# Mixers of a hybrid decoder layer: TensorE's order written by hand, substitution for two heads at a time

## The chip, the core and the metric

The kernel runs on one core of one Trainium2 chip, as one program. The metric is the time of one execution in microseconds of the device, as the median of several runs; a second number comes from one execution that was profiled. The core has a matrix engine (TensorE, PE in the profile; its weight loads are PEld), a vector engine (VectorE, DVE), a scalar engine (ScalarE, ACT), a general engine (GpSimd, POOL) and a queue from which the transfers are issued (SyncE, SP). Each works through its own instructions in their order and waits on semaphores for the others.

## What is computed

One layer of a decoder for 1,024 prompt tokens and 8 x 8 sampled tokens, all in 32-bit floats:

```
x = x + 1/2 * post1(SwiGLU_1(pre1(x)))
h = pre2(x); z = h @ w_in                       # q, k, v; conv q/k/v; z; a, b; two gates
A: sliding-window (128) attention, 8 heads of 64, 2 key/value heads, a sink per head
B: conv of width 4 on q/k/v + SiLU, gated DeltaNet (4 heads of 128), gated RMSNorm
m = (sigmoid(gA) * (oA @ w_branch_a) + sigmoid(gB) * (oB @ w_branch_b)) @ w_out
x = x + post2(m)
x = x + 1/2 * post3(SwiGLU_2(pre3(x)))
```

The delta net needs, for each head and each block of tokens, the solution of a unit lower triangular system: with `a = I + M`, `M` strictly lower, it uses the inverse of `a`. The state then goes through the blocks one after another (the recurrence).

## The kernel before

The residual stream lies transposed (features on partitions, tokens along the free axis) in three chunks of 384, 384 and 320 tokens (`CH`). A product in 32-bit precision is made of three faster ones: weights and activations are split into a high and a low piece (`split_w`: a cast on ScalarE at L113 and a subtraction on VectorE at L114), and `gemm` (lines 140 to 142) multiplies high by high, high by low and low by high. `unit(u)` loads and splits 128 columns of `w_in`; a unit for all three chunks is 3 x 8 x 3 = 72 products. The mixers have 32 such units behind the ones for attention's q, k, v: 12 convolutions (`conv_unit`), 4 for z (`z_unit`), 16 gates (`gate_unit`, `gate_do`). Their results go to memory (`zd`, `gd`) or to a head's tiles.

Instructions are put in order by a planner at build time: it simulates all engines, and on each engine takes the next instruction that it believes ready, earlier program text first; `high_priority` moves some ahead. It thus decides where TensorE does a projection between two steps of attention or of the delta net. Only in attention did the program add edges of its own (`chain`, "halves in turn").

`attention_prompt` goes through 16 items (8 blocks of 128 queries x 2 pairs of heads). `att_s` makes the scores, VectorE adds the mask (L862) and takes maxima (L822), ScalarE the exponentials (L828), then four ScalarE multiplications divide by the sum (L832). `att_o` transposes the probabilities (L883), ScalarE copies them (L888), and TensorE multiplies by the values (L893). `attention_sample` does four such items for the sampled tokens.

`delta_head(h, A, ps)` does one head. Two sets of eight tiles, `HA` and `YA`, serve heads 0, 2 and 1, 3; `YA` is also attention's. Its parts:

- transposes of k and their squares for the norm (L1075 to L1078), the decay matrices: differences on VectorE (L1105), exponentials on ScalarE (L1113, L1114), their transposes on TensorE (L1119); q.k products (L1102) and k.k products (L1122), which give `M` (L1126), the last block by L1138 to L1152;
- the inverse of the 32 x 32 diagonal blocks: the blocks go to memory and come back one to a partition (`bd`, L1161 to L1165), 34 partitions; 31 steps of a multiplication and a subtraction on VectorE (L1180, L1186); a transposed copy (L1189); blocks out (L1187, L1190) and, into zeroed tiles `L` and `U` (POOL, L1191 and L1192), ten transfers back (L1195 to L1198);
- the inverse of 128 from 32, on TensorE (L1211 to L1230), scalings (L1202, L1203), and `M` turned into what the recurrence needs (L1235);
- the recurrence over 8 blocks (L1253 to L1272), in each a chain PE, DVE, PE, DVE;
- the sampled tokens (L1282 to L1306) and the gated norm (L1313 to L1323), whose result goes to `obd`.

The order of the calls is: attention; convolutions and z of head 0; `delta_head(0)`; and so on, four heads, with gates between and after; the last four gates go chunk by chunk, so that the chunks of `xn2` come free one by one for the next stage, which loads `oad` and `obd` (L1367).

PSUM tiles are `pa` (3, projections), `ph` and `py` (2 each; `pb` takes them in turn) and `po` (1).

Of the kernel before, what the change touches and what calls it, by code (L numbers as in the profile page):

```python
# [35 lines left out]
def body(ctx: ExitStack, tc: tile.TileContext, d):  # L36
# [23 lines left out]
    bd = [dp.tile([34, 32, 32], F32, tag=f"bd{i}", name=f"bd{i}") for i in range(12)]  # L60
# [758 lines left out]
    def softmax(s3, sk, sm):  # L819
        j = s3.shape[1]  # L820
        m, neg, e, l, r = (sm[:, 4 * i : 4 * i + j] for i in range(5))
        nc.vector.tensor_reduce(out=m, in_=s3, op=ALU.max, axis=AX.X)  # L822
        nc.vector.tensor_tensor(out=m, in0=m, in1=sk, op=ALU.max)
        nc.vector.tensor_tensor(out=e, in0=sk, in1=m, op=ALU.subtract)
        nc.vector.tensor_scalar_mul(neg, m, -1.0)
        nc.scalar.activation(e, e, AF.Exp)
        for i in range(j):
            nc.scalar.activation(s3[:, i, :], s3[:, i, :], AF.Exp, bias=neg[:, i : i + 1], accum_out=l[:, i : i + 1])  # L828
        nc.vector.tensor_tensor(out=l, in0=l, in1=e, op=ALU.add)
        nc.vector.reciprocal(r, l)  # L830
        for i in range(j):
            nc.scalar.mul(s3[:, i, :], s3[:, i, :], r[:, i : i + 1])  # L832

    items = [(n, tp2) for n in range(8) for tp2 in range(2)]
    pos = {}
    masked = []
    SYNC = mybir.DependencyInfo(mybir.DependencyClass.Sync, mybir.DependencyReason.DATA)
    NOSYNC = mybir.DependencyInfo(mybir.DependencyClass.NoSync, mybir.DependencyReason.DATA)
    chain = []
    half2 = (slice(0, 64), slice(64, 128))  # L840

    def att_s(it):
        n, tp2 = items[it]
        k0 = 128 if n == 0 else 0
        ps = (ph(), py())
        for j in range(2):
            for g2, hs in enumerate(half2):
                mm = nc.tensor.matmul(
                    ps[g2][:, j * 256 + k0 : j * 256 + 256],
                    YA[tp2 * 2 + j][hs, n * P : n * P + P],  # L850
                    kT[hs, (n - 1) * P + k0 : (n + 1) * P],
                    start=True,
                    stop=True,
                )
                if masked:
                    tc.add_manual_dep(mm.ins, masked[-1], SYNC, reason="both halves start together")
                if chain:
                    tc.add_manual_dep(mm.ins, chain[-1], NOSYNC, reason="halves in turn")
                chain.append(mm.ins.name)
        s4 = sbs[it % 2][:, :1024].rearrange("p (h k) -> p h k", k=256)[:, :, k0:256]  # L860
        for g2 in range(2):
            mask = nc.vector.tensor_tensor(  # L862
                out=s4[:, 2 * g2 : 2 * g2 + 2, :],
                in0=ps[g2].rearrange("p (j k) -> p j k", k=256)[:, :, k0:256],
                in1=cst[:, C_AM + k0 : C_AM + 256].unsqueeze(1).to_broadcast([P, 2, 256 - k0]),
                op=ALU.add,
            )
        masked.append(mask.ins.name)
        softmax(s4, vec[:, V_SK + 4 * tp2 : V_SK + 4 * tp2 + 4], st())

    def att_o(it):
        n, tp2 = items[it]
        sb = sbs[it % 2]
        if n not in pos:
            pos[n] = po_tile()
        po = pos[n]
        h2s = (1,) if n == 0 else (0, 1)
        pt = (ph(), py())
        for g2 in range(2):
            for h2 in h2s:  # L880
                for j in range(2):
                    c0 = (2 * g2 + j) * 256 + h2 * P
                    mm = nc.tensor.transpose(pt[g2][:, h2 * 256 + j * P : h2 * 256 + j * P + P], sb[:, c0 : c0 + P], ident)  # L883
                    tc.add_manual_dep(mm.ins, chain[-1], NOSYNC, reason="behind the scores")
                    chain.append(mm.ins.name)
        ptb = pts[it % 2]
        copies = [
            nc.scalar.copy(ptb[:, g2 * 512 + h2s[0] * 256 : g2 * 512 + 512], pt[g2][:, h2s[0] * 256 : 512]) for g2 in range(2)  # L888
        ]
        for h2 in h2s:  # L890
            blk = n - 1 + h2
            for g2, hs in enumerate(half2):
                mm = nc.tensor.matmul(  # L893
                    po[hs, tp2 * 256 : tp2 * 256 + 256],
                    vtok[:, blk * P + hs.start : blk * P + hs.stop],
                    ptb[:, g2 * 512 + h2 * 256 : g2 * 512 + h2 * 256 + 256],
                    start=h2 == h2s[0],
                    stop=h2 == 1,
                )
                tc.add_manual_dep(mm.ins, copies[1].ins.name, SYNC, reason="both halves start together")  # L900
                tc.add_manual_dep(mm.ins, chain[-1], NOSYNC, reason="halves in turn")
                chain.append(mm.ins.name)
        if tp2 == 1:
            for t in range(4):
                nc.scalar.copy(YA[t][:, n * P : n * P + P], po[:, t * P : t * P + P])

    def attention_prompt():
        for it in range(len(items)):
            att_s(it)
            if it > 0:  # L910
                att_o(it - 1)
        att_o(len(items) - 1)
        for t in range(4):
            nc.sync.dma_start(oad[t, :, :NPR], YA[t][:, :NPR])

    def attention_sample():
        kc, vc = YA[5], YA[7]
        nc.sync.dma_start(vc[:, :NPR].rearrange("p (b c) -> p b c", c=P), d["vc"].rearrange("b k c -> k b c"))
        nc.sync.dma_start(kc[:, :NPR].rearrange("p (b c) -> p b c", c=P), d["kc"])
        pos = po_tile()  # L920
        for it in range(4):
            bg2, g2 = it // 2, it % 2
            lo, hi = 64 * g2, 64 * g2 + 64
            ps = py()
            for b4 in range(4):
                b = bg2 * 4 + b4
                ql = qs[lo:hi, b, :, :].rearrange("p t k -> p (t k)")
                nc.tensor.matmul(ps[32 * b4 : 32 * b4 + 32, 0:128], ql, kc[lo:hi, b * P : b * P + P], start=True, stop=True)
                nc.tensor.matmul(ps[32 * b4 : 32 * b4 + 32, 128:192], ql, kT[lo:hi, NPR:NT], start=True, stop=True)
            sb = YA[6][:, it * 256 : it * 256 + 192]  # L930
            nc.vector.tensor_tensor(out=sb[:, 0:128], in0=ps[:, 0:128], in1=cst[:, C_SMC : C_SMC + P], op=ALU.add)
            nc.vector.tensor_tensor(
                out=sb[:, 128:192], in0=ps[:, 128:192], in1=cst[:, C_SMN + bg2 * NSM : C_SMN + bg2 * NSM + NSM], op=ALU.add
            )
            softmax(sb.unsqueeze(1), vec[:, V_SKS + g2 : V_SKS + g2 + 1], st())
            pt = py()
            nc.tensor.transpose(pt[:, 0:128], sb[:, 0:128], ident)
            nc.tensor.transpose(pt[:NSM, 128:256], sb[:, 128:192], ident)
            ptb = YA[0][:, it * 256 : it * 256 + 256]
            nc.scalar.copy(ptb[:, 0:128], pt[:, 0:128])  # L940
            nc.scalar.copy(ptb[:NSM, 128:256], pt[:NSM, 128:256])
            nc.tensor.matmul(
                pos[lo:hi, bg2 * 128 : bg2 * 128 + 128], vts[:, lo:hi], ptb[:NSM, 128:256], start=True, stop=False
            )
            for b4 in range(4):
                b = bg2 * 4 + b4
                nc.tensor.matmul(
                    pos[lo:hi, bg2 * 128 + 32 * b4 : bg2 * 128 + 32 * b4 + 32],
                    vc[:, b * P + lo : b * P + hi],
                    ptb[:, 32 * b4 : 32 * b4 + 32],  # L950
                    start=False,
                    stop=b4 == 3,
                )
        obs = YA[1][:, :256]
        nc.vector.tensor_copy(
            obs.rearrange("p (t b k) -> p t b k", t=4, b=8), pos[:, :256].rearrange("p (b t k) -> p t b k", t=4, b=8)
        )
        nc.sync.dma_start(oad[:, :, NPR:NT].rearrange("t p q -> p t q"), obs.rearrange("p (t q) -> p t q", t=4))


    ncv = s2b.tile([P, 12, 3], F32, tag="ncv", name="ncv")
    nc.vector.memset(ncv, 0.0)

    def conv_unit(u, dst):
        w = unit(U_QKV + u, f"qkv{u}")
        cw = [vec[:, V_CW + u * 4 + j : V_CW + u * 4 + j + 1] for j in range(4)]
        for c, (a, b) in enumerate(CH):
# [4 lines left out]
            gemm(ps, w, xn2, c)  # L972
# [39 lines left out]
    eps4 = s2b.tile([P, 1], F32, tag="eps4", name="eps4")  # L1012
    nc.vector.memset(eps4, 4.0 * P * EPS * EPS)

# [324 lines left out]
    for i in range(0, 2):  # L1339
        gate_unit(i)  # L1340
# [210 lines left out]
```

## Time and profile before

| | |
|---|---|
| median of 3 runs | 2436.82 us (2432.78 to 2436.84) |
| profiled execution | 2440.89 us, span of its instructions 2439.1 us |
| PE busy / PEld busy | 2373.7 us (97%) / 2291.1 us (94%) |
| DVE / ACT / POOL busy | 1704.9 us (70%) / 1127.3 us (46%) / 50.9 us (2%) |
| mean granted TensorE clock | 0.989 |
| transfers | 264.67 MB, 109 GB/s |
| the mixers as treated here | 855 to 1478 us of the span |

Rows of a stretch give, for each engine, busy microseconds and the number of instructions in brackets, then the granted TensorE clock (PEclk, 1.00 is full), the busy share of the transfer engines and GB/s. Rows of a group give line, engine, operation, the tiles written and read, shapes and count, then busy time and the mean of one in ns, then the idle time just before and what ended it. Rows of waits give who waited for whom: microseconds in total, times, the longest. Rows of the timeline give start, duration, engine, line and operation. Matmuls overlap in the record, so PE's busy time is not PE at its peak.

### The profile page before, as it was taken

How to read it: one execution, taken by the hardware profiler on the slowest of the kernel's cores; microseconds unless marked ns; L12 is line 12 of the kernel's file. 1: busy time of each engine (PE TensorE's matmuls, PEld its weight loads, DVE VectorE, ACT ScalarE, POOL GpSimd, SP SyncE). 2: the span in 40 equal slices, each digit the busy share in tenths (PEclk: the TensorE clock that was granted, in tenths of full speed). 3: DMA queues.
4: the chain of work that ended last, by engine and by line, in shares of the span. 5: the costliest groups of instructions: out<-in, count | busy, mean ns of one | idle time of the engine just before them, and what ended most of it. 6: DMA issues, size and time to landing. Idle time of an engine off the chain costs nothing.

```text
span 2439.1 us, 38987 instructions
## 1 busy us (share of the span) xinstructions
PE 2373.7 (97%) x14535; PEld 2291.1 (94%) x14535; DVE 1704.9 (70%) x3519; ACT 1127.3 (46%) x2344; POOL 50.9 (2%) x36
## 2 busy tenths in 40 slices
PE   8999999999999999989999999999999999999997
PEld 7999999999998988888898899999999999999997
DVE  8887657757788576679697226556997576676677
ACT  7644423323465478634544333246654333233344
POOL 0000000000000000011111000000000000000000
PEclk9999999999999999999999999999999999999998
DMA  8332212213453311322223345435532122122453
GB/s 270 121 117 87 69 51 86 70 51 96 166 187 125 123 40 46 105 75 85 94 79 102 94 157 167 130 117 204 164 98 93 57 74 78 52 78 81 154 166 132
DMA packets 161558, 264.67 MB, mean 109 GB/s; under 512 B 35028, under 2 KB 66232, under 8 KB 161360
## 3 DMA queue, kind: packets, MB, share of 16 engines
q1 hardware_dynamic: 161368, 262.18, 33.3%
q8 instruction: 114, 1.87, 0.3%
q14 instruction: 76, 0.62, 0.1%
HBM read 223.88 MB, written 39.21 MB: 108 GB/s over the span
## 4 chain that ended last, share of the span: by engine, by line
PE 48%; DVE 6%; DMA 1%; ACT 1%; issue 1%; SPq 0%; POOL 0%; DVEq 0%; ACTq 0%; POOLq 0%
PE pa L140 7%; PE pa L142 7%; PE pa L141 7%; PE pa L464 4%; PE pa L465 4%; PE pa L466 4%; PE ph L346 2%; PE ph L347 2%; PE py L347 2%; PE py L346 2%; PE py L345 2%; PE ph L345 2%; DVE s L1186 1%; DVE s L1180 1%; DVE t L980 1%
## 5 line engine op out<-in xcount | busy, mean ns | idle before, releaser
L464 PE MATMUL pa<-ch,h_c_s 128*128 128x384 f32 x704 | 237.4, 337 | 4.3 <-DVE t L470 3.9
L465 PE MATMUL pa<-cl,h_c_s 128*128 128x384 f32 x704 | 236.4, 336 | 4.7 <-DVE cl L274 4.7
L466 PE MATMUL pa<-ch,l_c_s 128*128 128x384 f32 x704 | 236.3, 336 | 0.0
L470 DVE TENSOR_TENSOR t<-pa,t 128x384 f32<-128x384 f32 x308 | 170.0, 553 | 84.4 <-PE pa L466 84.3
L464 PE MATMUL pa<-ch,h_c_a 128*128 128x384 f32 x528 | 177.1, 335 | 1.2 <-ACT t L382 0.8
L466 PE MATMUL pa<-ch,l_c_a 128*128 128x384 f32 x528 | 176.7, 335 | 0.0
L465 PE MATMUL pa<-cl,h_c_a 128*128 128x384 f32 x528 | 176.6, 335 | 0.0
L113 ACT CAST h_c_a<-r_c_a 128x512 fp32r<-128x512 f32 x132 | 81.8, 620 | 131.5 <-PE pa L465 113.3
L464 PEld LDWEIGHTS pa<-ch,h_c_s 128*128 128x128 f32 x704 | 132.9, 189 | 7.9 <-DVE t L470 7.4
L465 PEld LDWEIGHTS pa<-cl,h_c_s 128*128 128x128 f32 x704 | 133.0, 189 | 4.9 <-DVE cl L274 4.9
L466 PEld LDWEIGHTS pa<-ch,l_c_s 128*128 128x128 f32 x704 | 132.9, 189 | 0.0
L113 ACT CAST h_c_s<-q_c_s 128x512 fp32r<-128x512 f32 x132 | 82.0, 621 | 106.4 <-PE pa L465 95.8
L140 PE MATMUL pa<-xbh,h_ga 128*128 128x384 f32 (+1 forms) x384 | 129.3, 337 | 0.0
L142 PE MATMUL pa<-xbh,l_ga 128*128 128x384 f32 (+1 forms) x384 | 128.8, 335 | 0.0
L141 PE MATMUL pa<-xbl,h_ga 128*128 128x384 f32 (+1 forms) x384 | 128.3, 334 | 0.0
L464 PEld LDWEIGHTS pa<-ch,h_c_a 128*128 128x128 f32 x528 | 99.1, 188 | 2.1 <-ACT t L382 1.1
L466 PEld LDWEIGHTS pa<-ch,l_c_a 128*128 128x128 f32 x528 | 99.1, 188 | 0.0
L465 PEld LDWEIGHTS pa<-cl,h_c_a 128*128 128x128 f32 x528 | 99.1, 188 | 0.0
L140 PE MATMUL pa<-xbh,h_qkv 128*128 128x384 f32 (+1 forms) x288 | 96.7, 336 | 0.0
L141 PE MATMUL pa<-xbl,h_qkv 128*128 128x384 f32 (+1 forms) x288 | 96.4, 335 | 0.0
L142 PE MATMUL pa<-xbh,l_qkv 128*128 128x384 f32 (+1 forms) x288 | 96.2, 334 | 0.0
L113 ACT CAST h_c_s<-r_c_s 128x512 fp32r<-128x512 f32 x44 | 27.4, 623 | 147.7 <-PE pa L465 135.7
(615 smaller groups left out, 7340.9 us busy)
## 6 DMA issues: line engine op xcount, KB each, us to landing
r_c_a<-in_up_dram SPq DMA_DIRECT2D x132, 256.0 KB
q_c_a<-in_up_dram SPq DMA_DIRECT2D x44, 256.0 KB
q_ub<-in_up_dram SPq DMA_DIRECT2D x44, 256.0 KB
r_ub<-in_up_dram SPq DMA_DIRECT2D x44, 256.0 KB
r_ua<-in_up_dram SPq DMA_DIRECT2D x42, 256.0 KB
q_ua<-in_up_dram SPq DMA_DIRECT2D x42, 256.0 KB
r_da<-in_dn_dram SPq DMA_DIRECT2D x40, 256.0 KB
q_da<-in_dn_dram SPq DMA_DIRECT2D x40, 256.0 KB
```

What stands on the lines that cost most here:

```text
L113: nc.scalar.copy(hi, full)
L140: nc.tensor.matmul(ps[:, :n], hi[:, j, :], at(xh, k), start=first, stop=False)
L141: nc.tensor.matmul(ps[:, :n], hi[:, j, :], at(xl, k), start=False, stop=False)
L142: mm = nc.tensor.matmul(ps[:, :n], lo[:, j, :], at(xh, k), start=False, stop=last)
L345: nc.tensor.matmul(ps[:, :n], hi[:, i, :], hh, start=i == 0, stop=False)
L346: nc.tensor.matmul(ps[:, :n], hi[:, i, :], hl, start=False, stop=False)
L347: nc.tensor.matmul(ps[:, :n], lo[:, i, :], hh, start=False, stop=i == len(hs) - 1)
L464: nc.tensor.matmul(ps, wh[:, k, :], xh[:, k, :], start=k == 0, stop=False)
L465: nc.tensor.matmul(ps, wh[:, k, :], xl[:, k, :], start=False, stop=False)
L466: nc.tensor.matmul(ps, wl[:, k, :], xh[:, k, :], start=False, stop=k == 3)
L470: nc.vector.tensor_tensor(out=out, in0=ps, in1=other, op=ALU.add)
L980: nc.vector.scalar_tensor_tensor(out=acc[:, :m], in0=pre[:, j : j + m], scalar=cw[j], in1=acc[:, :m], op0=ALU.mult, op1=ALU.add)
```

## The change

TensorE's instructions in the mixers are no longer ordered by the planner: inside `tc.manual_schedule` they run in the order of the program text. The other engines stay with the planner. The units become generators that yield after each of 24 steps (three products, an estimate of the time with it); `fill(us)` takes steps from the front of `queue` until their estimates reach `us`, and `finish` drains given units. The steps of attention and delta net are written with fills between them.

A head is now an object with `first` (up to `M`, its blocks on their way to memory, and the transposed values) and `second` (all from L1211's products on). Between them `invert` treats two heads in one: their blocks lie on 68 partitions, and the 31 steps are done once for both. The 32 x 32 inverses are written to their places in two arrays in memory (`ld`, `ud`) that were zeroed once at the start, and whole rows are read back, so that the zeroing of `L` and `U` goes. In the softmax the four ScalarE multiplications are one VectorE multiplication with a broadcast. Within `first` and `second` both halves of a head's blocks are worked on in turn (`Ds`, `Es`, `Xs`; a new tile `R2`), the scaling by `bgr` is one instruction for four blocks, the sampled tokens' value transpose moves to `first`, and the U.v product of a block is issued a block ahead (`uv`). 14 gates are in the queue, and the last two go chunk by chunk.

```diff
-    bd = [dp.tile([34, 32, 32], F32, tag=f"bd{i}", name=f"bd{i}") for i in range(12)]
+    bm, bu = ([dp.tile([34, 32, 32], ...) for h in range(4)] for n in ("bm", "bu"))
+    ld, ud = ([dp.tile([8, 4 * 4128], ...) for h in range(4)] for n in ("ld", "ud"))
...
-        for i in range(j):
-            nc.scalar.mul(s3[:, i, :], s3[:, i, :], r[:, i : i + 1])
+        nc.vector.tensor_tensor(out=s3, in0=s3, in1=r.unsqueeze(2).to_broadcast(list(s3.shape)), op=ALU.mult)
...
+    queue = []
+    def gemm_p(ps, w, c):
+        for k in range(KT):
+            gemm(ps, w, xn2, c, ks=(k,), ends=(k == 0, k == KT - 1))
+            yield 0.0013 * width(c) + 0.04
+    def fill(us):
+        while us > 0 and queue:
+            t = next(queue[0], None)
+            if t is None:
+                queue.pop(0)
+            else:
+                us -= t
...
-            gemm(ps, w, xn2, c)
+            yield from gemm_p(ps, w, c)
...
     def attention_prompt():
         for it in range(len(items)):
             att_s(it)
+            fill(1.0 if it else 4.0)
             if it > 0:
-                att_o(it - 1)
+                att_t(it - 1)
+                fill(1.8)
+                att_v(it - 1)
+                fill(1.0)
...
+    nc.gpsimd.memset(HA[5], 0.0)
+    for h in range(4):
+        for t in (ld, ud):
+            nc.sync.dma_start(t[h].rearrange("c (e x) -> (c e) x", x=1032), HA[5][:, :1032])
...
+    # Head.first: k transposes, norms, differences, exponentials; fill(3.0)
+    #   for each half: q.k products, decay transposes; fill(1.2)
+    #   for each half: k.k products, M; fill(0.6)
+    #   last block: products; fill(3.0); transpose; blocks of M to bm; v transposes
+    # Head.second: M.U of both halves; fill(0.6); L.X, X.L of both; fill(1.0); 64 x 64 corners,
+    #   fill(1.0), fill(1.0), fill(0.8), fill(0.8); fill(0.6); k.E of both halves; recurrence:
+            for c in range(8):
+                ...
+                if c > 0:
+                    nc.tensor.matmul(p[:, 0:128], M[:, cs], S, start=False, stop=True)
+                ...
+                    nc.tensor.matmul(po[:, 0:128], S, q[:, cs], start=True, stop=False)
+                fill(0.5)
+                nc.tensor.matmul(p[:, 128:256], k[:, cs], vns, start=True, stop=True)
+                ...
+                nc.tensor.matmul(po[:, 0:128], vn, QK[:, cs], start=c == 0, stop=True)
+                ...
+                    uv(c + 1)
+                    fill(0.5)
+    #   sampled tokens and norm with fill(1.0), fill(1.0), fill(1.5), fill(2.0) between
...
+    def invert(heads):
+        a, b = heads
+        Md, Ld = (t[:68, :NPR].rearrange("p (r s) -> p r s", s=32) for t in (a.A[7], b.A[7]))
+        for i, x in enumerate(heads):
+            nc.sync.dma_start(Md[34 * i : 34 * i + 34], bm[x.h])
+        ...   # 31 steps as before, on 68 partitions
+        nc.vector.tensor_copy(Md, Ld.rearrange("p r s -> p s r"))
+        for i, x in enumerate(heads):
+            h, L, U = x.h, x.A[1], x.A[5]
+            nc.sync.dma_start(blocks32(ud[h]), Md[34 * i : 34 * i + 32])
+            nc.sync.dma_start(bu[h][32:34], Md[34 * i + 32 : 34 * i + 34])
+            nc.sync.dma_start(blocks32(ld[h]), Ld[34 * i : 34 * i + 32])
+            nc.sync.dma_start(U[:, :NPR].rearrange("p (c s) -> p c s", s=P), whole_rows(ud[h]))
+            nc.sync.dma_start(L[:, :NPR].rearrange("p (c s) -> p c s", s=P), whole_rows(ld[h]))
+            ...   # two small blocks of the sampled tokens
+        fill(38.0)
...
+    with tc.manual_schedule(engines={mybir.EngineType.PE}):
+        queue += heads[0].conv + zs[0:2] + gates[0:2]
+        attention_prompt()
+        attention_sample()
+        finish(heads[0].conv + zs[0:2])
+        queue[:0] = heads[1].conv
+        heads[0].first()
+        finish(heads[1].conv)
+        queue += gates[2:]
+        heads[1].first()
+        invert(heads[0:2])
+        heads[0].second()
+        queue[:0] = heads[2].conv
+        heads[1].second()
+        finish(heads[2].conv)
+        queue[:0] = heads[3].conv
+        heads[2].first()
+        finish(heads[3].conv)
+        queue[:0] = zs[2:4]
+        heads[3].first()
+        invert(heads[2:4])
+        finish(zs[2:4])
+        heads[2].second()
+        heads[3].second()
+        finish(list(queue))
+        ...   # the last two gates, chunk by chunk
```

More of the change, by code (lines that the diff above doesn't have):

```diff
@@ L830, in softmax @@
         nc.vector.reciprocal(r, l)
-        for i in range(j):
[L832 to L910, printed above, removed]
-                att_o(it - 1)
[L912 to L958, printed above, removed]
@@ L964, in conv_unit, with finish @@
+    def finish(units):
+        for u in units:
+            if u in queue:
+                queue.remove(u)
+                drain(u)
     def conv_unit(u, dst):
@@ L1031, in gate_do @@
         ps = pa()
-        gemm(ps, w, xn2, c)
+        yield from gemm_p(ps, w, c)
         z = t1()
@@ new lines, in att_t @@
+    def att_t(it):
+        n, tp2 = items[it]
+        sb = sbs[it % 2]
+        h2s = (1,) if n == 0 else (0, 1)
+        pt = (ph(), py())
+        for g2 in range(2):
+            for h2 in h2s:
+                for j in range(2):
+                    c0 = (2 * g2 + j) * 256 + h2 * P
+                    nc.tensor.transpose(pt[g2][:, h2 * 256 + j * P : h2 * 256 + j * P + P], sb[:, c0 : c0 + P], ident)
+        ptb = pts[it % 2]
+        probs[it] = [
+            nc.scalar.copy(ptb[:, g2 * 512 + h2s[0] * 256 : g2 * 512 + 512], pt[g2][:, h2s[0] * 256 : 512]) for g2 in range(2)
+        ]
@@ L1165, in delta_head @@
[L1165 to L1173 removed]
+            M3 = M[:, :NPR].rearrange("p (c s) -> p c s", s=P)
@@ new lines, in invert @@
+        fill(38.0)
+    heads = [Head(h, (HA, YA)[h % 2]) for h in range(4)]
+    zs = [z_unit(h) for h in range(4)]
+    gates = [gate_unit(i) for i in range(14)]
+    with tc.manual_schedule(engines={mybir.EngineType.PE}):
[23 more added lines that the diff above has]
+        finish(list(queue))
+        wg4 = [unit(U_GA + i, f"ga{i}") for i in range(14, 16)]
+        for c in range(3):
+            for i in range(2):
+                drain(gate_do(14 + i, wg4[i], c))
```

659 lines of the change are left out of this document (388 added, 271 removed).

## The prediction

> **What bounds the kernel now.** I read the page first (busy time of each engine), then busy time by stretch of the mixers, then who TensorE waited for, then the order of time around one substitution.
>
> ```profile
> PE 2373.7 (97%) x14535; PEld 2291.1 (94%) x14535; DVE 1704.9 (70%) x3519; ACT 1127.3 (46%) x2344; POOL 50.9 (2%) x36
> ```
>
> TensorE (PE) is the bound: 97% busy, so 65 us of the span without it. Only what lies in the mixers can be won or lost by this change. The stretches are: attention of the prompt (855 to 988), attention of the sample and the first head's start (to 1018), then the delta heads to 1415, then gates alone.
>
> ```profile
> core 0: us, PE busy (x) PEld busy (x) DVE busy (x) ACT busy (x) POOL busy (x), PEclk, DMA share, GB/s
> 855.00:988.00 133.00, 129.86 (x854) 108.46 (x854) 88.25 (x263) 106.93 (x327) 0.00 (x0) 1.00 0.15 46
> 988.00:1018.00 30.00, 27.87 (x225) 23.81 (x223) 18.92 (x80) 16.92 (x50) 2.93 (x3) 0.89 0.35 111
> 1018.00:1085.00 67.00, 58.53 (x351) 55.90 (x350) 54.95 (x169) 29.87 (x58) 11.12 (x7) 0.92 0.24 70
> 1085.00:1160.00 75.00, 71.77 (x468) 64.04 (x467) 63.58 (x182) 35.79 (x79) 8.35 (x5) 0.99 0.32 101
> 1160.00:1233.00 73.00, 72.58 (x476) 64.82 (x475) 54.69 (x149) 37.80 (x85) 10.03 (x6) 0.99 0.29 95
> 1233.00:1300.00 67.00, 63.18 (x432) 58.83 (x430) 53.43 (x174) 34.19 (x82) 7.36 (x6) 0.97 0.21 60
> 1300.00:1360.00 60.00, 57.40 (x340) 52.81 (x339) 40.58 (x91) 19.34 (x36) 6.51 (x4) 0.97 0.38 120
> 1360.00:1415.00 55.00, 55.00 (x352) 47.89 (x351) 20.88 (x43) 23.56 (x54) 4.45 (x2) 1.00 0.30 96
> 1415.00:1478.00 63.00, 63.00 (x384) 63.00 (x383) 21.41 (x41) 23.95 (x51) 0.00 (x0) 1.00 0.57 185
> sum 623.00, PE 599.17 PEld 539.55 DVE 416.69 ACT 328.34 POOL 50.74; mean PE 66.57 PEld 59.95 DVE 46.30 ACT 36.48 POOL 5.64
> ```
>
> The last row shows where PE idles in these 623 us: 623.00 - 599.17 = 23.8 us, none of it after 1360. The column PEclk shows the second loss: the shortfall below 1.00, times each length, is 3.3 + 5.4 + 0.75 + 0.73 + 2.0 + 1.8 = 14 us of clock.
>
> ```profile
> 1056.10:1059.50 3.40, 3.40 (x16) 3.24 (x17) 2.40 (x12) 0.58 (x1) 0.00 (x0) 0.50 0.02 5
> 1059.50:1062.90 3.40, 0.68 (x6) 0.49 (x5) 3.40 (x10) 0.26 (x1) 2.22 (x2) 1.00 0.00 0
> 1062.90:1069.70 6.80, 4.77 (x20) 4.34 (x21) 6.80 (x24) 3.79 (x8) 2.37 (x1) 0.50 0.31 112
> ```
>
> These rows show the cost of a gap: after 3.4 us with PE busy for 0.68, the next 6.8 us ran at clock 0.50 with PE busy 4.77, so some 2.4 us of work was lost on top of the gap. Part of the 14 us fell into idle time; I count half, 7 us. What a better order could win is then 24 + 7 = 31 us, 1.3% of the time. The waits themselves:
>
> ```profile
> PE py L1119 <- ACT s L1114: 7.1, 2, 4.7
> PE py L1215 <- ACT s L1212: 3.2, 1, 3.2
> PE py L1211 <- DMA s<-bd: 2.6, 1, 2.6
> PE ph L883 <- ACT s L832: 2.5, 6, 0.6
> ```
>
> The longest is the decay chain at a head's start (transposes, differences, exponential, L1119); the substitution, whose blocks come back at L1211, costs PE only 2.6 us, because the planner had put convolutions and gates beside it.
>
> **The change part by part.**
>
> *Supply of filler.* A projection unit is 24 steps of three products. The stretch 1415 to 1478 is units alone (products of L142 only, a third of all):
>
> ```profile
> 855.00:988.00 133.00, 53.16 (x159) 29.97 (x159) 1.00 0.15 46
> ...
> 1415.00:1478.00 63.00, 41.55 (x128) 23.84 (x127) 1.00 0.57 185
> ```
>
> 128 of them in 63.00 us, so 24, a unit, in 11.8 us. fill counts a unit as 8 x (0.539 + 0.539 + 0.456) = 12.3 us, so fill(38.0) is 36.6 real us. All fills round up to whole steps: I count some 8 to 10 steps for an attention item, 162 to 175 in both attentions (the queue then holds 168), 23 in a head's first, 75 in invert, 47 in second. The 14 gates run out just as the last second ends. So no filler is spare: where a fill is too short, PE stands still.
>
> *invert, the new wait.* PE passes from the last pieces of head 1 (or 3) to fill(38.0) and then to second's first product, in fixed order. What must end under that fill I read from head 3 of before, where least lay in the way:
>
> ```profile
> 1290.93 0.24 PE L1149 MATMUL py<-eye,s 64*64 64x64 f32 x1
> 1291.76 0.79 SPq L1163 DMA_DIRECT2D bd<-s  x2
> 1295.05 0.24 SPq L1165 DMA_DIRECT2D s<-bd  x1
> 1300.37 0.20 DVE L1180 TENSOR_TENSOR s<-s,s 34x31 f32<-34x31 f32 x1 [0.68 <-DMA s<-bd]
> 1339.51 0.18 DVE L1186 TENSOR_TENSOR s<-s,s 34x31 f32<-34x31 f32 x1
> 1339.73 1.87 DVE L1189 COPY s<-s 34x1024 f32<-34x1024 f32 x1
> 1341.63 0.24 SPq L1190 DMA_DIRECT2D bd<-s  x1
> 1344.63 0.81 SPq L1195 DMA_DIRECT2D s<-bd  x2
> 1350.29 0.94 SPq L1198 DMA_DIRECT2D s<-bd  x2
> 1352.06 1.15 PE L1211 MATMUL py<-s,s 128*128 128x128 f32 x8 [2.60 <-DMA s<-bd]
> ```
>
> From the last transpose to the first step of the substitution: 1300.37 - 1290.93 = 9.4 us (blocks out, blocks in). The substitution: 39.3 us, much of it other work on VectorE (DVE). Copy: 1.9. From the copy's end to PE: 1352.06 - 1341.60 = 10.5.
>
> ```profile
> L1180 DVE TENSOR_TENSOR s<-s,s 34x31 f32<-34x31 f32 (+15 forms) x124 | 43.4, 350 | 3.0 <-DMA s<-bd 1.4
> L1186 DVE TENSOR_TENSOR s<-s,s 34x31 f32<-34x31 f32 (+15 forms) x124 | 42.9, 346 | 1.6
> L114 DVE TENSOR_TENSOR l_ga<-r_ga,h_ga 128x512 fp32r<-128x512 f32 x26 | 17.6, 681 | 6.8 <-ACT h_ga L113 6.6
> ```
>
> For a pair the 62 steps stay as long (the same elements in each partition, 68 partitions in place of 34): (43.4 + 42.9) / 4 = 21.6 us, and no longer twice per pair, so DVE saves 43 us in all; DVE is not the bound, so that alone is worth nothing. Beside it runs the gates' DVE work, 2.5 units x 2 splits x 0.68 = 3.4 us and a little, and small gaps: 28 us as an estimate. The way back has two large transfers in place of ten and no memset between (L, U start from zeros in memory): writes in 128-byte pieces, then 512-byte rows. The nearest rows are L1190 to L1195, 3.0 us until a write was seen, and L1198 to L1211, 1.8 us for the last read; the reads are larger now. I take 7, between 4.8 and 10.5. Sum: 9.4 + 28 + 1.9 + 7 = 46.3 us, against a cover of 36.6 + 1 us of value transposes. PE waits 8.7 us, and 2.4 us of work is lost to the clock, twice: **+21** (with 23 and 4.8 as ends: 0 and a little; with 33 and 10.5: +38).
>
> *Attention.* ScalarE loses L832, DVE gets one wide multiplication an item. The width's nearest row is L147:
>
> ```profile
> L147 DVE TENSOR_TENSOR s<-s,s 128x1088 f32<-128x1088 f32 x4 | 5.1, 1275 | 1.8 <-ACT s L146 1.8
> L822 DVE TENSOR_REDUCE st<-s 128x4 f32<-128x1024 f32 x14 | 17.0, 1213 | 0.1
> L862 DVE TENSOR_TENSOR s<-ph,cst 128x512 f32<-128x512 f32 x14 | 9.6, 684 | 2.9 <-PE py L848 2.8
> L980 DVE SCALAR_TENSOR_TENSOR t<-t,vec,t 128x384 f32<-128x384 f32 x25 | 15.2, 607 | 2.2 <-ACT t L978 2.2
> ```
>
> 1.2 us x 16 = 19 us more on DVE, to 88 + 19 = 107 in some 125 us. While the first three units in the queue are convolutions (nine L980 each and as much again in small operations, some 11 us of DVE for 11.8 us of PE), an item asks DVE for 2 x 0.68 + 1.2 + 1.2 + 0.8 of small ones and 0.36 unit x 11 = 8.5 us, and PE for 4.2 of fill and 3.4 of its own (133 us less 159 / 24 units x 11.8, over 16): 7.6. For about eight items DVE is 0.9 us short each: 7 us. Four buffers of raw convolution rows could hide it (0); if each softmax came 1.2 us late it would be 19. I take **+7**.
>
> *Head starts and second.* The chain behind L1119 has fill(3.0) and four products, 4 us, as cover; before it cost 7.1 in all. I take 1.5 a head, **+6** (0 to 12). Second: the waits at L1215 and its like were 3 to 4; its recurrence has one or two steps of fill between products. **+6** (2 to 15), most in head 1, where convolutions share DVE.
>
> *Finishing.* finish(conv) runs units back to back, DVE about as long as PE: +2. The tail has two gate units by chunk (23.6 us) in place of four, over the last head's end:
>
> ```profile
> L1317 PE MATMUL py<-s,eye x12: 275/591/592, 1209.3 to 1399.8; 128*128 128x512 f32 x8, 128*128 128x64 f32 x4
> L1323 SPq DMA_DIRECT2D obd<-s x4: 319/320/338, 1147.6 to 1413.6; - x4
> ```
>
> 14 us to the write, then a write, a read, and splits, some 20 us: just hidden, +1. A few more changes between step and filler than before: +2 (0 to 5). The eight zero fills (4 MB) fall where the DMA share is 0.15, and SP and POOL have room: 0, covered by loads that are a unit ahead; without that cover the first filler waits up to 10 us.
>
> Sum: 21 + 7 + 6 + 6 + 2 + 1 + 2 = 45 new, 31 gone: +14 us. Made against the profiled run's own 2440.89 us (span 2439.1): 2455. That run lay 4 us over the median of 2436.8, so **2451**.
>
> **The rivals.**
>
> *The pair's substitution fits (faster).* If the chain under fill(38.0) takes at most 37.6 us, the 21 go, and 24 - 31 = -7: 2430. For it: 21.6 us of steps is far less than the 39 elapsed before, and 10.5 us of return had ten issues in it. Against: the 9.4 us of blocks out and in are still there. It decides at 37.6 us.
>
> *PE has hidden slack (faster by more).* Weight loads (PEld) are busy 539.55 of 623.00, so 83 us lack them, against 23.8 without PE. If a third of the other 59 were dependent products that steps between them cure, -20 on top: 2410. Against: the small products of attention and delta net are among them, which stay. The Trainium skill, Perfetto Trace Analysis, section Identifying the Most-Contended Engine, says matmul busy time hides headroom and weight-load busy share shows it; by that rule the mixers hold 83 us. The trace here agrees that the two differ, and cannot say how much can go.
>
> *Small pieces and softmax (slower by more).* If the 128-byte writes take 3 us longer in each pair and attention costs 19: +14 + 6 + 12: 2469. Against: L1165 was issued 2.5 us after the last such write of before. The Trainium skill, DMA: Bandwidth & Descriptors, Specifications, puts line rate at 512 bytes and more, with read-modify-write below; by that rule the new writes are the slow kind. The trace bounds it only for 4 pieces of 32 KB.
>
> *Nothing changes.* Waits only trade places (0 to 5 either way): 2437.
>
> **How the numbers follow.** Two thousandths of the time, 4.9 us, is what a measurement can tell. Chances: my sum 0.42 (own range 2442 to 2470), the worse form 0.12, the fitting pair 0.25, the hidden slack 0.07, no change 0.14. So slower 0.54, same 0.14, faster 0.32. The range goes from 2410 (hidden slack) to 2478 (all upper ends of invert and attention).
>
> **What would show it.** In the changed kernel: PE waiting at the first product of second for a DMA, 5 to 13 us, twice, with clock 0.50 behind it; DVE near full in the first 70 us of attention and PE waiting there for the softmax; 31 substitution steps twice, not four times; waits behind the decay exponentials under 2 us each. The sum is wrong if the two invert waits are under 2 us, or if the idle sum of the mixers drops below 15 us.

## The result, and the profile after

The changed kernel took 2445.89 us (median of five runs, 2443.45 to 2454.15) against 2433.80 for the kernel before on the same chip: ratio 1.0053, 95% interval 1.0033 to 1.0073. It is 12 us slower, 5 us less than forecast (2451), and on the forecast side.

First the engines' busy time, from the page of the changed kernel:

```profile
span 2445.9 us, 38715 instructions
PE 2368.8 (97%) x14535; PEld 2289.7 (94%) x14535; DVE 1690.5 (69%) x3385; ACT 1102.7 (45%) x2276; POOL 41.5 (2%) x33
```

TensorE is busy 4.9 us less than before and the span is 6.8 us longer in these two executions, so its idle time grew by 11.7 us, from 65.4 to 77.1. All of that is in the mixers. This is the same stretch of both kernels, busy time by stretch, before first and then after (TensorE's busy time is the second number, PEclk the granted clock):

```profile
800.00:1560.00 760.00, 736.17 (x4696) 672.82 (x4696) 492.34 (x1370) 367.48 (x891) 50.74 (x32) 0.98 0.31 96
```
```profile
800.00:1560.00 760.00, 724.81 (x4645) 664.48 (x4644) 472.50 (x1225) 340.85 (x820) 40.27 (x28) 0.98 0.34 105
```

Idle 23.8 us before, 35.2 after: 11.4 us more, close to the 12 us between the medians. The clock did not change in sum: it is 0.98 in both, and its shortfall below 1.00, added up in slices of 3.4 us, is 13.6 us in both. Who TensorE waited for, in the changed kernel (us in total, times, longest; rows from elsewhere in the program left out):

```profile
PE ph L1243 <- DMA s<-ud: 12.6, 2, 6.7
PE ph L979 <- DVE s L833: 8.7, 5, 2.6
...
PE py L1173 <- ACT s L1134: 3.0, 1, 3.0
PE py L1321 <- ACT s L1317: 2.9, 7, 0.6
PE pa L142 <- DVE t L1480: 2.5, 1, 2.5
...
PE ph L1250 <- ACT s L1244: 1.8, 3, 0.8
```

The first row is the first product of a head's second half, which waits for the inverted blocks to come back; the second is attention, whose transposes wait for the softmax division that now stands on VectorE. Before, the longest was L1119 with 7.1 us, and the blocks cost 2.6.

The way around the substitution, in order of time, for the second pair (start, duration, engine, line; idle time before and what ended it in brackets):

```profile
1301.41 0.24 PE L1210 MATMUL ph<-eye,R 64*64 64x64 f32 x1
...
1302.23 0.78 SPq L1220 DMA_DIRECT2D bm<-s  x2
...
1306.22 0.25 SPq L1397 DMA_DIRECT2D s<-bm  x1
...
1311.73 0.21 DVE L1403 TENSOR_TENSOR R<-s,s 68x31 f32<-68x31 f32 x1 [2.67 <-DMA s<-bm]
...
1337.97 0.19 DVE L1409 TENSOR_TENSOR s<-s,R 68x31 f32<-68x31 f32 x1
1338.19 1.13 DVE L1410 COPY s<-s 68x1024 f32<-68x1024 f32 x1
1339.35 0.33 SPq L1413 DMA_DIRECT2D ud<-s  x1
...
1341.51 0.38 SPq L1416 DMA_DIRECT2D s<-ud  x1
...
1346.51 2.05 PE L1243 MATMUL ph<-s,s 128*128 128x128 f32 x8 [6.66 <-DMA s<-ud]
```

From the start of the last transpose of the first half to the first step: 10.3 us. The 62 steps: 26.4. Copy: 1.1. Return: 7.2. Sum 45.1 (the four are rounded), or 44.9 from the end of that transpose. From there the filler lasted 38.2 us (1346.51 - 6.66 - 1301.65), and TensorE stood still for the rest. Behind each of the two waits, and at three other places, the clock fell to half:

```profile
851.40:858.20 6.80, 6.08 (x24) 5.34 (x25) 2.82 (x13) 2.90 (x13) 0.00 (x0) 0.50 0.16 45
1110.80:1117.60 6.80, 4.94 (x21) 4.97 (x22) 0.25 (x1) 1.42 (x3) 0.00 (x0) 0.50 0.83 194
1247.40:1250.80 3.40, 3.40 (x14) 3.40 (x12) 3.40 (x10) 3.35 (x6) 1.28 (x1) 0.51 0.02 5
1342.90:1349.70 6.80, 3.19 (x15) 3.22 (x16) 0.25 (x1) 0.35 (x1) 0.00 (x0) 0.50 0.84 196
1486.30:1489.70 3.40, 3.16 (x10) 3.16 (x11) 2.47 (x6) 1.39 (x3) 0.00 (x0) 0.50 0.96 313
```

Only the second and the fourth, behind the two waits, are in the prediction; the others are the start of attention, one head's start and the tail.

### The profile page after: what moved, and what is told of

Its sections match the earlier page's. It is cut to its first block, busy times and chain, and to the rows that moved or that the text cites. A ratio compares the mean times of both kernels' runs of the same rounds, so it can differ in the third digit from the quotient of the medians.

```text
span 2445.9 us, 38715 instructions
## 1 busy us (share of the span) xinstructions
PE 2368.8 (97%) x14535; PEld 2289.7 (94%) x14535; DVE 1690.5 (69%) x3385; ACT 1102.7 (45%) x2276; POOL 41.5 (2%) x33
## 4 chain that ended last, share of the span: by engine, by line
PE 81%; DVE 8%; DMA 5%; ACT 3%; issue 2%; SPq 0%; POOLq 0%; POOL 0%; DVEq 0%; ACTq 0%
PE pa L142 11%; PE pa L143 10%; PE pa L144 10%; PE pa L466 8%; PE pa L467 8%; PE pa L468 8%; PE py L349 3%; PE py L348 3%; PE ph L348 3%; PE ph L349 3%; PE ph L347 3%; PE py L347 3%; DVE R L1403 1%; DVE s L1409 1%; DMA q_da<-in_dn_dram 1%
## 5 line engine op out<-in xcount | busy, mean ns | idle before, releaser
L142 PE MATMUL pa<-xbh,h_ga 128*128 128x384 f32 (+1 forms) x384 | 134.7, 351 | 0.0
```

What stands on the lines that cost most here:

```text
L142: nc.tensor.matmul(ps[:, :n], hi[:, j, :], at(xh, k), start=first, stop=False)
```

## The experiments

The first question was whether the order costs the time, or what is ordered. All ratios are against the kernel before on the same chip; the changed kernel stands at 1.0053.

**The planner in place of the hand order.** The block that fixes TensorE's order is taken away; every instruction stays.

```diff
-    with tc.manual_schedule(engines={mybir.EngineType.PE}):
+    if True:
```

> The changed kernel with TensorE's order left to the planner; pairs, softmax on VectorE, zero fills and the two large transfers stay. If the hand order is what costs (its fixed fill of 38 us ends before the substitution of a pair): the planner puts other units beside it, the two waits at the first product of the second half go from 12.6 us in sum to under 4, and the time is about that of before, 2434 +- 5 us. If the pair itself costs (two heads wait for one substitution, and there is no other work in the program to put beside it): the waits stay at 10 us or more and the time stays at 2446 +- 5.

Measured: 2409.03 us, 0.9898 (0.9882 to 0.9914), 26 us under the kernel before. Both cases of the expectation had it too slow. Busy time by stretch of this kernel, whole and in the two places of the substitution:

```profile
1100.00:1120.00 20.00, 19.96 (x160) 19.24 (x159) 6.14 (x11) 7.59 (x20) 0.00 (x0) 1.00 0.58 151
...
1320.00:1340.00 20.00, 19.96 (x160) 19.42 (x159) 6.23 (x11) 6.78 (x17) 0.00 (x0) 1.00 0.63 170
```
```profile
800.00:1560.00 760.00, 751.75 (x4871) 695.10 (x4870) 490.22 (x1262) 354.75 (x846) 41.20 (x28) 0.99 0.35 111
```

Idle 8.3 us, against 35.2 by hand. The substitutions are no shorter here (the first takes 25.7 us from its first step to its copy, in both kernels); TensorE is simply never out of other work beside them. So the hand order costs 1.0053 - 0.9898 = 1.6%, 38 us, and what the change holds besides it is a gain.

**Which part of the hand order.** It is kept for the two attentions alone, then for the delta heads alone.

```diff
+        with tc.manual_schedule(engines={mybir.EngineType.PE}):
             attention_prompt()
             attention_sample()
```

> The changed kernel with the hand order kept in the two attentions alone; the delta heads are the planner's. With the planner everywhere the time was 2409, with the hand order everywhere 2446: 37 us. By the idle time of TensorE in 840 to 1000 (8.8 us in the hand order, 1.4 with the planner) and the half clock from 851 to 858 (3.4 us), attention's order costs some 11 us: 2420 +- 4. If nearly all of it is in the waits for the substitution, it stays at 2411 +- 3.

> The changed kernel with the hand order in the delta heads alone, attention left to the planner: the other side of the split. The two invert waits (12.6 us), the half clock behind them and the small waits of the second halves make the rest of the 37 us, some 26: 2435 +- 4. If the two parts do not add (the planner, free in attention, takes units that the hand order then lacks in the second halves), it is 2443 or more.

Measured: attention alone 2422.40, 0.9945 (0.9928 to 0.9962); delta heads alone 2437.51, 1.0009 (0.9997 to 1.0022). Over the planner's 0.9898 that is 11.4 and 27.0 us, together 38.4, where both at once cost 37.7: they add within their intervals, as expected. TensorE's longest wait in each, attention first:

```profile
PE ph L979 <- DVE s L833: 8.8, 5, 2.6
```
```profile
PE ph L1243 <- DMA s<-ud: 12.4, 2, 6.8
```

Each kernel has the wait of its own part, as long as in the changed kernel, and not that of the other.

**More filler beside the substitution.**

```diff
-        fill(38.0)
+        fill(46.0)
```

> The hand order with fill(46.0) in place of fill(38.0) beside each substitution. The two invert waits (12.6 us) and the half clock behind them (2 x 2.4 us) go, -17 us; but the gates run out 16 us of filler earlier, and the last second half stands bare: some ten steps of its chain at 1 to 1.5 us each, +12. Sum -5: 2441 +- 4. If the end can do without filler (its chain is short), 2430 +- 3; if the waits only move, wait for wait, 2446 +- 3.

Measured: 2449.49, 1.0051 (1.0033 to 1.0068): no change from 1.0053, the third case (by the ratio; the median lies 0.5 us above that case's range). The waits of this kernel show why:

```profile
PE py L1321 <- ACT s L1317: 6.5, 13, 0.8
...
PE ph L1250 <- ACT s L1244: 5.0, 4, 3.6
...
PE py L1383 <- DVE s L1371: 2.1, 1, 2.1
...
PE ph L1243 <- DMA s<-ud: 1.4, 1, 1.4
```

The wait for the blocks went from 12.6 to 1.4 us: the cover was what it lacked. The second halves paid for it: in 1360 to 1480 TensorE is now busy 108.32 us of 120, after 117.72, with 10.2 us at half clock:

```profile
1360.00:1480.00 120.00, 108.32 (x664) 92.62 (x664) 45.83 (x82) 50.76 (x115) 8.86 (x4) 0.94 0.32 104
```
```profile
1446.40:1456.60 10.20, 7.96 (x10) 3.17 (x11) 4.10 (x6) 1.80 (x2) 0.26 (x1) 0.50 0.33 100
```

**Filler at the start of attention.** The transposes of decays and values move into the ordered block, with filler between.

```diff
+        fill(1.5)
         psc = pb()          # transposes of the decays
...
+        fill(1.0)           # then the transposes of the values
...
+        fill(1.0)
         attention_prompt()
```

> The changed kernel with some 3.5 us of filler between the last decay products, the transposes of the values and the first scores, which the hand order had shut out there. If the half clock from 851.4 to 858.2 comes from the small products and gaps of that place: it goes, and with it some 3.4 us of work and 1 us of idle time: 2441.5 +- 2. If the clock falls whatever is placed there, or the filler is missed later (the gates run out that much earlier): 2446 +- 2.

Measured: 2450.13, 1.0069 (1.0053 to 1.0084): no gain. The median is above both cases, but the interval overlaps that of the changed kernel (1.0033 to 1.0073), so a loss is not shown. The half clock at 851 is gone; it is back at two later places:

```profile
877.40:884.20 6.80, 5.53 (x20) 5.30 (x20) 3.40 (x10) 3.65 (x12) 0.00 (x0) 0.50 0.01 2
1000.30:1014.00 13.70, 11.77 (x60) 8.96 (x61) 4.59 (x25) 5.00 (x18) 0.00 (x0) 0.50 0.29 93
```

The second is the attention of the sample, where the queue now runs dry: from 997.3 to 1012.4 TensorE does no step of a unit. Both this and the longer fill say the same: the sum of filler is fixed and used up, and in a fixed order a piece moved to one step is missed at another.

**The three convolutions of attention spread out.** They alternate chunk by chunk with two z units and a gate unit.

```diff
-        queue += heads[0].conv + zs[0:2] + gates[0:2]
+        lead = [mixed(co[0], zs[0]), mixed(co[1], zs[1]), mixed(co[2], gates[0])]
+        queue += lead + gates[1:2]
```

> The changed kernel with the filler of attention in another order: the three convolution units of head 0 alternate, chunk by chunk, with two z units and a gate unit, in place of coming first. If VectorE is short only while convolutions follow each other: the waits behind the softmax multiplication (8.7 us) fall under 3 us and the time by 5 to 7 us, to 2440 +- 3. If VectorE's total is short, or the later end of the convolutions holds up head 0's start: the waits move to 940 to 1010 and the time stays at 2446 +- 3.

Measured: 2446.37, 1.0049 (1.0034 to 1.0064): no change. The wait behind VectorE fell, but one for the softmax's exponentials on ScalarE took its place:

```profile
PE ph L982 <- DVE s L833: 4.2, 3, 2.0
PE ph L982 <- ACT s L830: 3.8, 1, 3.8
```

8.0 in place of 8.7 us. Part of the idle time moved back, as the second case says: TensorE is busy 74.78 us of 80 in 860 to 940, after 71.26 in the changed kernel, but 66.50 of 70 in 940 to 1010, after 70.00.

**The softmax division back on ScalarE**, under the hand order and then under the planner.

```diff
-        nc.vector.tensor_tensor(out=s3, in0=s3, in1=r.unsqueeze(2).to_broadcast(list(s3.shape)), op=ALU.mult)
+        for i in range(j):
+            nc.scalar.mul(s3[:, i, :], s3[:, i, :], r[:, i : i + 1])
```

> The changed kernel, hand order and all, with the softmax division alone back on ScalarE (four multiplications an item). Under the hand order TensorE waits 8.7 us behind the division on VectorE (L833), in the stretch 860 to 940 where VectorE is busy 66 us of 80. If VectorE's load in that stretch sets the wait (the prediction's step for attention): some 12 us leave VectorE there, the wait falls under 3 us and the time by 5 to 7 us, to 2440 +- 3. If the fixed order does (the transposes of an item come at a set place, whoever does the division, and the chain of the softmax is as long on ScalarE): 6 us or more stay, behind L834 on ScalarE, and the time stays at 2446 +- 3.

> The planner's order, with the softmax division back on ScalarE (four multiplications an item in place of one wide one on VectorE). In 855 to 988 VectorE is busy 102.0 us of 133 and ScalarE 82.9 with the planner; this moves some 19 us from the one to 24 on the other, as in the kernel before (88 and 107), and TensorE has 1.4 us of idle time there to lose or win. If neither engine is then short: 2409 +- 2.5. If VectorE's load is what held the hand order up and still matters here: 2405. If ScalarE's longer chain per item shows: 2413 or more.

Measured under the hand order: 2441.42, 1.0027 (1.0014 to 1.0040), 4.5 us less by the medians and 6.3 by the ratios: the first case. The intervals of the two kernels just overlap, but TensorE's idle time in 800 to 1560 agrees, with 28.0 us after 35.2. The wait of 8.7 us became

```profile
PE ph L980 <- ACT s L834: 2.0, 2, 1.1
```

Under the planner: 2408.38, 0.9901 (0.9878 to 0.9925), the same as with the division on VectorE. Busy time in 855 to 988 of the two, ScalarE's division first:

```profile
855.00:988.00 133.00, 131.61 (x897) 108.14 (x897) 87.53 (x262) 107.64 (x334) 0.14 (x1) 1.00 0.21 72
```
```profile
855.00:988.00 133.00, 131.62 (x881) 107.84 (x880) 101.98 (x271) 82.94 (x265) 0.15 (x1) 1.00 0.21 69
```

VectorE at 88 or at 102 us: TensorE is as busy. The wait at L979 needed both, the division on VectorE and an order that could not step past it.

**One substitution for each head**, under the planner.

```diff
-        a, b = heads
-        Md, Ld = (t[:68, :NPR].rearrange("p (r s) -> p r s", s=32) for t in (a.A[7], b.A[7]))
+        for x in heads:
+            h, L, U = x.h, x.A[1], x.A[5]
+            Md, Ld = (t[:34, :NPR].rearrange("p (r s) -> p r s", s=32) for t in (x.A[7], U))
...
+            fill(19.0)
```

> The planner's order again, with the substitution undone into one for each head (34 partitions, twice per pair, 43 us more on VectorE in all); the blocks still go by the two large transfers, and everything else stays. If the pair brings what the planner's kernel gains over the kernel before (26 us): 2430 or more. If it does not (VectorE is no bound, and other units stand beside either form): 2409 to 2415, and the gain is the new order of the program's steps.

Measured: 2416.60, 0.9922 (0.9905 to 0.9939): 6 us over the pair by the ratios, 8 by the medians, just above the second case. The two intervals overlap a little, so the loss is near the limit of what is told apart here; TensorE's idle time in 800 to 1560 points the same way, 15.2 us after 8.3:

```profile
800.00:1560.00 760.00, 744.83 (x4844) 688.80 (x4843) 524.56 (x1394) 352.60 (x843) 41.70 (x28) 1.00 0.35 111
```

So the pair is probably a gain, of about a quarter of the planner's 26 us. The edit also moves the steps' buffers: they use the head's own `L` and `U` here, which are loaded only when the steps and the writes of their results are done. The run does not tell this from the pairing.

**The planner with no filler in the text.** fill() places nothing; each unit stands whole where finish() asks for it.

```diff
-        while us > 0 and queue:
+        while False and us > 0 and queue:
```

> The planner's order with no filler between the steps in the program's text: each unit stands whole where finish() asks for it, as in the kernel before. If the gain of the planner's kernel over before that is not the pair's (18 of 26 us) comes from the text, whose order the planner takes as its first wish: 2425 to 2432, with waits back in the head starts. If it comes from the rest (steps in two halves, more buffers for the decays, transfers, softmax): 2409 to 2413.

Measured: 2447.09, 1.0056 (1.0036 to 1.0075): 38 us lost against the planner's kernel, worse than either case. This text is not that of the kernel before, as the expectation has it. There the text has the first gates behind head 1, and the planner drew some of them ahead, to head 0; here all gates stand behind the last head. So two things change at once, the filler between the steps and the place of the gates. When the results of the gates were written to memory, in the kernel before and in this one (the two numbers before the semicolon are the first and the last start):

```profile
L1040 SPq DMA_DIRECT2D gd<-t x48: 319/326/1462, 1069.3 to 1475.9; - x48
```
```profile
L931 SPq DMA_DIRECT2D gd<-t x48: 319/320/632, 1243.4 to 1487.7; - x48
```

No gate stood beside the first substitution. TensorE ran out of work there, and the half clock behind that lasted 20.5 us:

```profile
PE ph L1243 <- DMA s<-ud: 13.6, 1, 13.6
```
```profile
1069.80:1090.30 20.50, 7.77 (x35) 7.51 (x36) 5.02 (x15) 1.42 (x3) 0.00 (x0) 0.50 0.62 154
```

That the planner leans on the order of the text is shown. How much of the 38 us is the filler between the steps, and how much the place of the gates, is not.

**The square's buffer**, under the planner: the squares of the second four blocks of k to columns of their own.

```diff
-                nc.scalar.activation(M[:w, : n * P], pt[:w, : n * P], AF.Square)
+                sq = M[:w, c0 * P : c0 * P + n * P] if c0 < 8 else M[:w, :P]
+                nc.scalar.activation(sq, pt[:w, : n * P], AF.Square)
```

> The planner's order with one buffer apart: the squares of the second four transposed blocks of k go to their own columns, in place of those that VectorE's sum still reads. In the planner's trace ScalarE's second square waits 2.67 us for that sum at 1223, TensorE waits 3.04 us behind it for its buffer, and 3.4 us at half clock follow. If that chain is what ends last there, wait and half clock go: -4.5 us, 2404.5 +- 2. If another wait stands right behind it (VectorE is busy 18.8 of 20 us there): 2408 to 2410.

Measured: 2409.11, 0.9898 (0.9877 to 0.9920): no change, the second case. In order of time, the planner's kernel, and then this one:

```profile
1223.45 0.60 ACT L1134 ACTIVATE s<-py 128x512 f32<-128x512 f32 x1 [2.67 <-DVE nk L1135]
...
1224.10 1.22 PE L1173 MATMUL py<-s,s 128*128 128x128 f32 x4 [3.04 <-ACT s L1134]
```
```profile
1220.97 0.27 ACT L1135 ACTIVATE s<-ph 64x128 f32<-64x128 f32 x1 [3.99 <-DVE nk L1136]
...
1221.30 1.11 PE L1176 MATMUL ph<-eye,s 128*128 128x128 f32 x4 [3.13 <-ACT s L1135]
```

The third, small square still shared columns with the first, so it waited in the second one's place, and TensorE with it. The sum on VectorE (L1136) comes late in either.

**A shorter way around the substitution.** The 64-column block before the k.k products, and U's load ahead of the other writes.

```diff
+            # block 8: products, decay, transpose and M, ahead of k.k
             for j, c0 in enumerate((0, 4)):
                 pk = pb()
...
             nc.sync.dma_start(blocks32(ud[h]), Md[34 * i : 34 * i + 32])
+            nc.sync.dma_start(U[:, :NPR].rearrange("p (c s) -> p c s", s=P), whole_rows(ud[h]))
             nc.sync.dma_start(bu[h][32:34], Md[34 * i + 32 : 34 * i + 34])
```

> The changed kernel with a shorter way around the substitution: in a head's first half the 64-column block is done before the k.k products, so that its two small writes no longer come last, and on the way back the load of U is issued right behind the write of its blocks, ahead of the other writes. Same work, same fill. If the chain under the fill sets the two invert waits: some 3 us go from the start (1068.3 to 1064.9) and 1 to 2 us from the return, the waits fall from 12.6 us in sum to 3 to 5, and the time by 8 to 10 us, to 2437 +- 3. If the steps on VectorE or the transfer times absorb the earlier start (they end when they end): the waits stay at 10 to 13 and the time at 2446.

Measured: 2445.72, 1.0050 (1.0035 to 1.0064): no change, and the question is not answered. The block took its fill(3.0) along, so the large writes went behind that filler, and the first pair's blocks came in no earlier:

```profile
1066.91 0.80 SPq L1221 DMA_DIRECT2D bm<-s  x2
...
1069.49 1.81 SPq L1219 DMA_DIRECT2D bm<-s  x4
...
1072.88 0.26 SPq L1398 DMA_DIRECT2D s<-bm  x1
```

1072.88 against 1072.31. In the second pair they were asked for 1.5 us earlier (1304.70 against 1306.22), yet the wait was no shorter (7.03 after 6.66), since the filler ended earlier too (1338.15 against 1339.85). SP's order of the return, which is the planner's, stayed as it was. Whether a shorter chain would give back its length was not settled by this run.

No kernel here beats the planner's by more than the measurement tells. That one beats both kernels of the case.

## Why the prediction was right, and where it was not

*Sign and place: right.* The largest new wait stands where it was put, twice, with the clock at 0.50 behind it. The sum for the second pair: blocks out and in 10.3 (said 9.4), steps 26.4 (28), copy 1.1 (1.9), return 7.2 (7), in all 45.1 (46.3); cover 38.2 (37.6). Wait 6.66 and 5.91 where 8.7 was said, 12.6 us in sum for 17.4. At half clock TensorE was busy 4.94 and 3.19 us behind them, which is some 4.1 us of work lost, so the whole term measures about 16.7 us. Two sums of the prediction are off by a little: twice 8.7 + 2.4 is 22.2 and not 21, and the upper end of its range comes to 2480 and not 2478. The substitution of 68 partitions took as long per step as that of 34 (medians of 354 and 353 ns beside means of 350 and 346). The fitting pair as a rival fell by its own condition, and the longer fill showed that it had a second fault: covering the chain gives no 21 us while the filler is finite. That no filler was spare stood in the prediction's own first step.

*Attention: right in size.* 8.7 us behind L833, said 7; the division put back took 4.5 off the time. The prediction laid the shortage to the three convolutions at the head of the queue. Spreading them halved the wait behind VectorE (4.2 us) but brought one behind ScalarE, so they are not the whole cause: what ends the wait for good is the division off VectorE, or an order that can step past it. VectorE was less full than "near full", 66 us of 80 in 860 to 940.

*Smaller terms.* Head starts 3.0 (said 6), all of it in one head, and not behind the exponentials of the decays, where "under 2 us each" was said and no wait shows: TensorE waited there for a PSUM buffer that ScalarE's square (L1134) still read. Second halves 2.9 + 1.8 and some single ones of 1, about 6 (6); tail 2.5 (1), which the planner's kernel has too (2.4). Missed: the start of attention, some 1 us idle and 6.8 us at half clock, since the fixed order let no filler in before the first scores. That cost some 4 us, about as much as the substitution came out below its 21, so the near hit of the whole sum is in part luck.

*The 31 us "gone": right in the sum, credited to the wrong part.* The prediction took the idle time before as what a better order of TensorE wins. In the changed kernel the former waits are indeed gone or smaller, and most of the 35.2 us of idle time is new. But the planner's run shows whose gain that was. The same program without the hand order has 8.3 us of idle time and a clock shortfall of 6.8 us, after 23.8 and 13.6 in the kernel before, so the other edits together win their 26 us without it. The hand order adds 26.9 us of idle time and 6.8 us of clock to that, 38 us in all with the medians, and gives nothing that shows. The 7 us of clock that the prediction counted as gone are still there: of the 13.6 us after, half lies at the two waits of the substitution, and half at the start of attention, one head's start and the tail. So the net sum was right with one term that belonged to another part of the change.

*"DVE saves 43 us, worth nothing alone".* Worth perhaps 6 to 8 us, by the kernel with single substitutions under the planner, although VectorE is not the bound on average. Why it costs that (the second head's blocks come a substitution later, the buffers of the steps are others, or VectorE is short in single places) was not tried apart.

*The hidden slack.* The planner's kernel landed on that rival's time, 2410, but not by its mechanism. TensorE busy without weight loads in 800 to 1560 is 63.4 us before, 60.3 after, 56.7 with the planner; its idle time went from 23.8 to 8.3 us and the clock's shortfall from 13.6 to 6.8 us. The Trainium skill, Perfetto Trace Analysis, section Identifying the Most-Contended Engine, would look for headroom in the weight loads' share; here more than half of what was won was plain idle time, which the busy share of TensorE does show.

*Small pieces.* The load of U was issued 2.2 us after the write of its 128-byte pieces, and the return took 7.2 us, as estimated, not 3 more. The Trainium skill, DMA: Bandwidth & Descriptors, Specifications, puts such pieces below line rate; nothing here was long enough to show that.

*Open:* how the 18 to 20 us of the planner's gain that are not the pair's divide among the interleaved text, the place of the gates in it, the head in two halves and the transfers.

## What to carry to other kernels

When an order is fixed by hand together with other edits, run the same program with the order left free: here the edits were worth 26 us and the order cost 38, and the net told neither. A fixed amount of filler has to be right at every step at once, and where all of it is used, lengthening one fill only moves the wait (12.6 us to 1.4 in one place, as much back in another). Write the filler into the program's text between the dependent steps, and let a planner decide when it runs: with none there, and the gates at the end of the text, the planner's kernel lost 38 us as well.

## What was not expected of the hardware

The clock can halve with no idle time in front of it that the record shows. In the profiled execution of the planner's kernel TensorE is busy for the whole of these 3.40 us, and for all 11.50 us from 840.00 on, yet the clock is at half, behind 2.5 us of very small products:

```profile
851.50:854.90 3.40, 3.40 (x16) 3.27 (x15) 0.28 (x1) 1.39 (x4) 0.00 (x0) 0.51 0.23 81
```
```profile
847.83 0.30 PE L773 MATMUL ph<-tk_g,cst 128*128 128x32 f32 x2
...
848.82 1.05 PE L778 MATMUL ph<-cst,tk_g 64*128 64x8 f32 x8
```

The kernel with the planner and ScalarE's division has the same products there and kept the full clock, so they alone do not decide it:

```profile
840.00:860.00 20.00, 20.00 (x137) 18.91 (x136) 10.32 (x33) 9.48 (x25) 0.00 (x0) 1.00 0.30 100
```
